# First norm in two VectorE operations and one of ScalarE a tile; last norm's sums gathered in PSUM

## The chip, the core and the metric

The kernel runs on one core of a Trainium2 chip. The metric is the device time of one execution in microseconds (us); of the kernel before three runs are shown. The core's engines run side by side, each through its own queue in program order: TensorE (PE; its weight loads are PEld), VectorE (DVE), ScalarE (ACT), GpSimd (POOL), and SyncE (SP), which here only issues DMAs. Matmul results land in PSUM, eight banks of 128 x 512 floats; everything else lies in SBUF.

## The reference

A decoder trunk of two layers over x (1024 tokens by 1024 channels, batch 1), conditioned by a vector c:

```python
c_act = jax.nn.silu(c)
for l in range(DEPTH):                                  # DEPTH = 2
    shift, scale, gate = jnp.split(c_act @ ada_w[l] + ada_b[l], 3, axis=-1)
    if l == 0:
        h = modulate(rmsnorm(x, norm_g[l]), shift, scale)   # h * (1 + scale) + shift
        y = pool_mixer(h, a_w_in[0], a_w_group[0], a_scale[0], a_w_out[0])
    else:
        kb, vb = shared_kv_blocks(x, c_act, kv_norm_g, kv_ada_w, kv_ada_b, w_kv)
        h = modulate(rmsnorm(x, norm_g[l]), shift, scale)
        y = swa_sink_mixer(h, kb, vb, pos_bias, mask, b_w_in[0], b_sinks[0], b_w_out[0])
    x = x + gate[:, None, :] * y
return rmsnorm(x, final_g)
```

`pool_mixer` projects h to u and z, takes causal means of u over 2, 4, 8 or 16 tokens by channel group, mixes each group by a matrix, gates with silu(z) and projects back. `swa_sink_mixer` is windowed attention with sinks. All is float32.

## The kernel before

x is kept transposed: channels on the 128 partitions, in eight tiles k (`xk[k]`), tokens along the row, in two halves q of 512. A float32 factor is split into a high part, rounded to fp32r, and a low part, the remainder; a product is three fp32r matmuls (high times high, high weight times low activation and so on), accumulated in PSUM.

The stage that the change touches is the head, up to 88.6 us. It has these parts.

- Joined weights. For the first channel group the input projection and the group matrix are multiplied on the chip beforehand (`join_mm`, `split_wg`, `split_wu`, loads `fetch_c`, four pieces c0 to c3). The eight 128 x 512 results lie in PSUM banks `jb[0..7]`; `joined_h` (ScalarE) and `joined_l` (VectorE) write their high and low parts to SBUF. For m = 2, 3, 6 and 7 `joined_raw` (ScalarE) copies the bank to SBUF and `joined_sub` (GpSimd) subtracts from the copy.
- Statistics. `square2` (ScalarE) and `add2` (VectorE, for three tiles GpSimd) sum the squares of x over k for each q, `fold` closes the sum. `rstd_stats` sums over the partitions on TensorE into bank "o", VectorE writes `v` (L144), GpSimd raises it to the power of -0.5 (L149), and `rstd_spread` (L156) spreads the factors over the partitions into bank "tp"; ScalarE copies them to `rbs[q]`.
- adaLN. `dots` multiplies and sums two 128 x 1024 tiles of `ada_w` with silu(c), spread over the partitions in `cact` (L241 on VectorE), for shift and scale of one k, and `mod_scale` (L260) joins scale and norm_g to a column of `acol`. The spreading of c is a matmul of a row of ones with c, split in two fp32r parts (`onesr`, `crow`, L453).
- Modulation and first matmuls. `first_xn` multiplies x by the norm factor (L179), `first_h` writes the high part of h on ScalarE (L161), h itself over x (L372) and the low part on GpSimd (L373); for k = 0 `soon_h` and `soon_l` do the last two on VectorE (L378, L383). `first_mm` (L396) is a block of twelve matmuls for one k and q: four with the high parts, four with the low weight, four with the low activation. There are sixteen blocks, in the order k = 0, 4, 1, 5, 2, 6, 3, 7. The banks of q = 0 are those of `jb[0..3]`, the others "tp", "o" and those of `jb[6..7]`.

In this stage the order of every engine's queue is that of the source (`manual_schedule` over all engines). The loads of SP are in the same order; a load into a tile in use waits, with all loads behind it.

After the head, `block_sums` (L612, L613, L615) forms sums and differences of the h tiles that the later products need, four a j, while TensorE runs the first gates (L216). Later stages touch none of the changed code but the last: there the output projection's last half is done in two quarters of 256 tokens, each followed by `stats_quarter`, which sums two partial squares (`sq` and `more`) with `rstd_stats`: two matmuls for `sq` (L140, each recorded as two passes), `v` (L144), two for `more`, an addition (L147), the power (L149). A tile `fill` of `CONST_FILL` columns lies behind the constants in SBUF.

## Time and profile before

| | us |
|---|---|
| median of 3 runs | 996.78 (995.62 to 997.03) |
| profiled execution | 997.35 |
| its span | 995.6 |
| TensorE busy in the span | 971.3 (98%) |
| VectorE busy | 784.8 (79%) |
| ScalarE busy | 468.2 (47%) |
| GpSimd busy | 178.9 (18%) |

The span runs from the first to the last instruction that the profile shows; the execution's time is a little longer. Busy shares are means over the whole span, and matmuls overlap, so a busy TensorE need not be at its peak. The granted clock of TensorE is 1.00 at 2.4 GHz and 0.50 at 1.2 GHz. In a row of the timeline the first number is the start, the second the duration; what stands in brackets is the idle time before it and what ended it. "PE ps_d" is a matmul into a bank of tag d.

### The profile page before, as it was taken

The page shows a single profiled execution, that of the slowest core. Times are in us where ns is not written, and L with a number is a line of the kernel's source. Part 1 is how long each engine was busy: PE and PEld are TensorE (multiplying, and loading weights), DVE is VectorE, ACT ScalarE, POOL GpSimd, SP SyncE. Part 2 cuts the span into 40 slices and gives each one's busy share as a digit, 9 for nine tenths or more (in the row PEclk, how much of TensorE's full clock was granted, in tenths as well). Part 3 has the DMA queues.
Part 4 walks back from the last instruction along what each step waited for, and adds up shares of the span by engine and source line. Part 5 has one row for each costly group of instructions (what it writes and reads, how often), then busy time and mean ns, then how long its engine had stood idle before and what let it go on. Part 6 is the DMA issues. An engine that isn't in the chain of part 4 may idle for free.

```text
span 995.6 us, 12704 instructions
## 1 busy us (share of the span) xinstructions
PE 971.3 (98%) x4530; PEld 801.7 (81%) x4530; DVE 784.8 (79%) x1405; ACT 468.2 (47%) x912; POOL 178.9 (18%) x194
## 2 busy tenths in 40 slices
PE   8899999999999999999999999999999999999996
PEld 6677888888888887888888886877788888887786
DVE  6998977767997699676782358699899878889995
ACT  6545534423343344551121134486767555666534
POOL 3652000000000000000000000043334212336723
PEclk9899999999999999999999999999999999999999
DMA  8462532164116410779871212412212221223222
GB/s 313 155 212 106 170 106 71 56 233 148 58 49 233 147 54 32 257 270 339 294 234 64 86 43 85 138 53 85 65 64 85 85 77 61 76 78 113 85 86 85
DMA packets 40625, 125.67 MB, mean 126 GB/s; under 512 B 4465, under 2 KB 6641, under 8 KB 40434
## 3 DMA queue, kind: packets, MB, share of 16 engines
q1 hardware_dynamic: 40416, 123.82, 36.8%
q10 hardware_dynamic: 146, 1.05, 0.3%
q8 instruction: 35, 0.57, 0.2%
q14 instruction: 28, 0.23, 0.1%
HBM read 111.22 MB, written 13.63 MB: 125 GB/s over the span
## 4 chain that ended last, share of the span: by engine, by line
PE 72%; DVE 20%; ACT 3%; issue 2%; POOL 1%; DMA 0%; POOLq 0%; DVEq 0%; SPq 0%; ACTq 0%
PE ps_d L216 13%; PE ps_d L657 10%; PE ps_S L216 8%; PE ps_d L207 5%; PE ps_d L205 5%; PE ps_d L206 5%; PE ps_S L657 4%; PE ps_o L216 4%; PE ps_tp L216 3%; DVE wl L121 3%; PE ps_o L657 2%; PE ps_tp L657 2%; PE ps_d L396 2%; DVE tmp L572 1%; DVE ad L241 1%
## 5 line engine op out<-in xcount | busy, mean ns | idle before, releaser
L119 ACT CAST wh<-raw 128x1024 fp32r<-128x1024 f32 x80 | 83.7, 1046 | 109.1 <-PE ps_d L216 66.6
L121 DVE TENSOR_TENSOR wl<-raw,wh 128x1024 fp32r<-128x1024 f32 x80 | 103.0, 1288 | 39.5 <-ACT wh L119 35.5
L205 PE MATMUL ps_d<-hm,wh 128*128 128x512 f32 x288 | 113.9, 396 | 1.1 <-ACT wh L119 1.1
L207 PE MATMUL ps_d<-hm,wl 128*128 128x512 f32 x288 | 112.7, 391 | 1.4 <-DVE wl L121 1.4
L206 PE MATMUL ps_d<-hm,wh 128*128 128x512 f32 x288 | 112.4, 390 | 0.0
L216 PE MATMUL ps_d<-gh,wh 128*128 128x512 f32 x224 | 82.1, 390 | 0.0
L241 DVE CUSTOM_DVE_ANT_0 tmp<-tmp,cact,pk 128x1024 f32<-128x1024 f32 x48 | 60.8, 1283 | 26.7 <-DMA tmp<-ada_rest 26.5
L207 PEld LDWEIGHTS ps_d<-hm,wl 128*128 128x128 f32 x288 | 54.1, 188 | 14.4 <-DVE wl L121 3.0
L216 PE MATMUL ps_S<-gh,wh 128*128 128x512 f32 x192 | 64.6, 390 | 0.0
L657 PE MATMUL ps_d<-hs,ws 128*128 128x512 f32 x264 | 64.0, 391 | 0.0
L205 PEld LDWEIGHTS ps_d<-hm,wh 128*128 128x128 f32 x288 | 54.1, 188 | 11.7 <-ACT wh L119 1.7
L1129 ACT ACTIVATE pt<-pt,nm 128x129 f32<-128x129 f32 x128 | 50.2, 395 | 26.5 <-DVE nm L1125 24.3
L206 PEld LDWEIGHTS ps_d<-hm,wh 128*128 128x128 f32 x288 | 54.2, 188 | 9.9
L657 PEld LDWEIGHTS ps_d<-hs,ws 128*128 128x128 f32 x264 | 49.6, 188 | 10.8
L564 POOL MEMSET tmp<- 128x16 f32 x16 | 1.7, 112 | 291.3 <-DVE tmp L572 129.7
L657 PE MATMUL ps_d<-ha,ws 128*128 128x512 f32 x216 | 52.9, 393 | 0.0
L633 ACT CAST ws<-tw 128x512 fp32r<-128x512 f32 x44 | 26.7, 621 | 54.7 <-PE ps_tp L216 15.2
L572 DVE TENSOR_TENSOR tmp<-tmp 128x1039 f32<-128x1039 f32 (+3 forms) x40 | 49.4, 1235 | 2.0 <-ACT tmp L693 0.9
L149 POOL TENSOR_TENSOR rs<-v,mhalf 128x4 f32<-128x4 f32 (+1 forms) x7 | 7.0, 996 | 237.3 <-DVE v L144 218.2
L216 PEld LDWEIGHTS ps_d<-gh,wh 128*128 128x128 f32 x224 | 42.0, 188 | 8.9
L657 PEld LDWEIGHTS ps_d<-ha,ws 128*128 128x128 f32 x216 | 40.7, 188 | 9.2
L216 PE MATMUL ps_d<-gh,wl 128*128 128x512 f32 x112 | 43.6, 390 | 0.0
(301 smaller groups left out, 2537.2 us busy)
## 6 DMA issues: line engine op xcount, KB each, us to landing
tmp<-ada_rest SPq DMA_DIRECT2D x48, 512.0 KB, 4.6
raw<-wb SPq DMA_DIRECT2D x32, 512.0 KB, 3.3
raw<-wa SPq DMA_DIRECT2D x28, 512.0 KB, 3.5
raw<-wao SPq DMA_DIRECT2D x20, 512.0 KB, 4.2
x<-xT SPq DMA_DIRECT2D x32, 256.0 KB, 6.0
ad<-ada_first SPq DMA_DIRECT2D x16, 512.0 KB, 4.4
raw<-wbo SPq DMA_DIRECT2D x16, 512.0 KB, 3.3
kept_g<-tmp SPq DMA_DIRECT2D x14, 512.0 KB, 2.8
```

What stands on the lines that cost most here:

```text
L119: nc.scalar.copy(out=wh, in_=raw)
L121: nc.vector.tensor_sub(out=wl, in0=raw, in1=wh.bitcast(F32))
L205: mm(ps, lh, acts(k, 0), start=k == 0, stop=False)
L206: mm(ps, lh, acts(k, 1), start=False, stop=False)
L207: mm(ps, ll, acts(k, 0), start=False, stop=k == n - 1)
L216: mm(p, lhs, acts(k, hl, q), start=start and k == 0 and s == 0, stop=stop and k == n - 1 and s == 2)
L241: nc.vector.tensor_tensor_reduce(out=raw, in0=raw, in1=ca, scale=0.5, scalar=pk[:, bcol:bcol + 1], op0=ALU.mult, op1=ALU.add, accum_out=ad ...
L396: mm(psu[i, q], w0[k // 2][:, k % 2, w, i * P:(i + 1) * P], block(k, q)[hl], start=k == 0 and s == 0, stop=k == KT - 1 and s == 2)
L572: nc.vector.tensor_add(out=nx[:, 2 * s - 1:], in0=cur[:, 2 * s - 1:], in1=cur[:, s - 1:PAD + T - s])
L633: nc.scalar.copy(out=ws[i][:, 0, :], in_=src)
L657: mm(ps, lhs, acts(k, hl), start=start and k == 0 and s == 0, stop=k == 3 and s == 2, skip_group_check=True)
L1129: nc.scalar.activation(pt[:, i, :P + 1], pt[:, i, :P + 1], AF.Exp, bias=nm[:, i:i + 1], scale=-1.0, accum_out=den[:, i:i + 1])
```

## The change

- `rstd_stats` with a second tile accumulates both groups of sums in the same PSUM columns; the addition of the second (L147) is gone.
- c is spread by one float32 matmul a half, from `ones` and `cact`; `crow` and `onesr` are gone.
- `joined_raw` and `joined_sub` are gone: all eight low parts of the joined weights are `joined_l` on VectorE. All additions of squares are on VectorE.
- The tile `xn` is gone. `first_h` multiplies x by the column of `acol` and by the norm factor in one VectorE operation, in place, and ScalarE adds the shift while rounding the high part. `first_l` adds the shift and subtracts the high part in one VectorE operation. What stays in x is h without its shift, so `block_sums` adds the shifts (columns of `adac`, and their sums in `acol[:, 24:28]`).
- The column of `acol` is made by ScalarE (Identity with scale and bias) instead of L260.
- Order: the loads of x tiles 4 to 7 of q = 0 come before those of c3, and `fetch_ada(0)` before the last four x tiles. The low parts and matmuls of a k stand one k later in the loop. `dots(4)` stand behind the second norm factor, and its spreading behind `first_mm(0, 0)`.
- `acol` has 28 columns and `CONST_FILL` is 44.

```diff
-CONST_FILL = 56
+CONST_FILL = 44
...
-    acol = cp.tile([P, 24], F32, name="acol")
+    acol = cp.tile([P, 28], F32, name="acol")
...
-        def sums(t, c0):
+        for i, t in enumerate((sq,) if more is None else (sq, more)):
             for j in range(n):
-                mm(st[:, c0 + j:c0 + j + 1], t[:, j * P:(j + 1) * P], invd, start=True, stop=True)
-
+                mm(st[:, j:j + 1], t[:, j * P:(j + 1) * P], invd, start=i == 0 and j == 0,
+                   stop=j == n - 1 and (i == 1 or more is None))
         v = sp.tile([P, 8], F32, tag="v", name="v")
-        sums(sq, 0)
         nc.vector.tensor_scalar_add(out=v[:, :n], in0=st[:, :n], scalar1=EPS)
-        if more is not None:
-            sums(more, n)
-            nc.vector.tensor_add(out=v[:, :n], in0=st[:, n:2 * n], in1=v[:, :n])
         rs = sp.tile([P, 8], F32, tag="rs", name="rs")
         nc.gpsimd.tensor_tensor(out=rs[:, :n], in0=v[:, :n], in1=mhalf[:, :n], op=ALU.pow)
...
-        crow = hp.tile([P, 2, T], F32R, tag="h", name="crow")
-        onesr = sp.tile([P, H], F32R, tag="xn", name="onesr", bufs=5)[:, :P]
-        nc.vector.tensor_copy(out=onesr[0:1, :], in_=ones[0:1, :].broadcast_to([1, P]))
...
-        def joined_raw(*ms):
...
-            for m in ms:
-                if m % 2 == 0:
-                    copies[m // 2] = tmp()
-                nc.scalar.copy(out=copies[m // 2][:, half(m % 2)], in_=jb[m])
...
-        def joined_sub(*ms):
-            for m in ms:
-                w = w0[m // 2][:, m % 2]
-                nc.gpsimd.tensor_sub(out=w[:, 1, :], in0=copies[m // 2][:, half(m % 2)],
-                                     in1=w[:, 0, :].bitcast(F32))
...
         def dots(k, i):
             ada_dot(ads[k][i], cact, 8 * i + k, C_ADAB + 8 * i + k)
             if i:
-                mod_scale(k, 8 + k, C_NG + k, 1)
-
-        xns = {}
-
-        def first_xn(k, q):
-            xns[k, q] = xn_tile(k, q, rbs[q])
+                g = pk[:, C_NG + k:C_NG + k + 1]
+                nc.scalar.activation(acol[:, k:k + 1], adac[:, 8 + k:9 + k], AF.Identity,
+                                     bias=g, scale=g)
...
         def first_h(k, q):
-            a, b, h, l = first_parts(k, q)
-            mod_h(xns[k, q], a, b, h)
-            nc.scalar.activation(first_f(k, q), xns[k, q], AF.Identity, bias=b, scale=a)
-            nc.gpsimd.tensor_sub(out=l, in0=first_f(k, q), in1=h.bitcast(F32))
-
-        def soon_h(k, q):
+
             a, b, h, _ = first_parts(k, q)
-            mod_h(xns[k, q], a, b, h)
-            nc.vector.tensor_scalar(out=first_f(k, q), in0=xns[k, q], scalar1=a, scalar2=b,
-                                    op0=ALU.mult, op1=ALU.add)
-
-        def soon_l(k, q):
-            _, _, h, l = first_parts(k, q)
-            nc.vector.tensor_sub(out=l, in0=first_f(k, q), in1=h.bitcast(F32))
+            nc.vector.scalar_tensor_tensor(out=first_f(k, q), in0=first_f(k, q), scalar=a,
+                                           in1=rbs[q], op0=ALU.mult, op1=ALU.mult)
+            nc.scalar.activation(h, first_f(k, q), AF.Identity, bias=b, scale=1.0)
+
+        def first_l(k, q):
+            _, b, h, l = first_parts(k, q)
+            nc.vector.scalar_tensor_tensor(out=l, in0=first_f(k, q), scalar=b,
+                                           in1=h.bitcast(F32), op0=ALU.add, op1=ALU.subtract)
...
-        def square2(n, q):
...
-        def add2(n, q, eng=None):
-            s = sq2[q][n % 2]
-            (eng or nc.vector).tensor_add(out=s, in0=s, in1=sqs[n, q])
+        def squares(q, *ks):
+
+            for n in ks:
...
+                nc.scalar.activation(sqs[n, q], xk[n][:, half(q)], AF.Square)
...
+        def adds(q, *ks):
+            for n in ks:
+                s = sq2[q][n % 2]
+                nc.vector.tensor_add(out=s, in0=s, in1=sqs[n, q])
...
             fetch_x(0, range(4))
             fetch_c(2)
+            fetch_x(0, range(4, 8))
             fetch_c(3)
-            fetch_x(0, range(4, 8))
-            fetch_x(1, range(8))
+            fetch_x(1, range(4))
             fetch_ada(0)
+            fetch_x(1, range(4, 8))
             fetch_ada(4)
...
-            nc.vector.tensor_copy(out=crow[0:1, 0, :], in_=cact[0:1, :])
-            nc.vector.tensor_sub(out=crow[0:1, 1, :], in0=cact[0:1, :],
-                                 in1=crow[0:1, 0, :].bitcast(F32))
             for i in range(3):
                 join_all(0, s=(i,))
             for q in range(2):
-                for i in range(2):
-                    mm(cbs[q], onesr[0:1, :], crow[0:1, i, half(q)], start=i == 0, stop=i == 1)
+                mm(cbs[q], ones[0:1, :].broadcast_to([1, P]), cact[0:1, half(q)],
+                   start=True, stop=True)
             split_wg(1)
             split_wu(1)
-            for k in range(4):
-                square2(k, 0)
-            for k in range(2, 4):
-                add2(k, 0)
+            squares(0, 0, 1, 2, 3)
+            adds(0, 2, 3)
...
+            squares(0, 4, 5, 6, 7)
+            adds(0, 4, 5, 6, 7)
+            squares(1, 0, 1, 2)
             join_all(3, (4, 5))
-            rs = rstd_stats(sq2[0][0], 4)
+            rs = rstd_stats(fold(0), 4)
             joined_h(4, 5)
             joined_l(4, 5)
-            square2(3, 1)
+            squares(1, 3)
             join_all(3, (0,))
-            add2(2, 1)
-            add2(3, 1, nc.gpsimd)
-            square2(4, 1)
+            adds(1, 2, 3)
             joined_h(0)
             join_all(3, (1,))
+            dots(0, 0)
+            joined_l(0)
             bc = rstd_spread(rs, 4)
-            square2(5, 1)
-            joined_l(0)
+            nc.scalar.copy(out=rbs[0], in_=bc)
             joined_h(1)
-            add2(4, 1)
-            add2(5, 1, nc.gpsimd)
-            nc.scalar.copy(out=rbs[0], in_=bc)
+            squares(1, 4, 5)
+            dots(0, 1)
             join_all(3, (2, 3))
-            square2(6, 1)
+            adds(1, 4, 5)
             joined_l(1)
-            square2(7, 1)
-            dots(0, 0)
-            add2(6, 1, nc.gpsimd)
+            squares(1, 6, 7)
+            adds(1, 6, 7)
+            sq = fold(1)
+            first_h(0, 0)
             joined_h(2, 3)
-            joined_raw(2, 3)
-            dots(0, 1)
-            add2(7, 1)
-            fold(1)
-            joined_sub(2)
+            joined_l(2, 3)
+            first_l(0, 0)
             jb += [bank("S") for _ in range(2)]
             for ci in range(4):
                 join_mm(6, jb[6], ci)
             for ci in range(3):
                 join_mm(7, jb[7], ci)
-            first_xn(0, 0)
-            soon_h(0, 0)
-            rs = rstd_stats(sq2[1][0], 4)
-            soon_l(0, 0)
+            rs = rstd_stats(sq, 4)
             joined_h(6)
-            joined_raw(6)
-            joined_sub(3)
-            dots(4, 0)
-            dots(4, 1)
             join_mm(7, jb[7], 3)
+            first_mm(0, 0)
             bc = rstd_spread(rs, 4)
-            first_mm(0, 0)
             nc.scalar.copy(out=rbs[1], in_=bc)
-            first_xn(0, 1)
-            soon_h(0, 1)
+            joined_l(6)
             joined_h(7)
-            joined_raw(7)
-            soon_l(0, 1)
-            joined_sub(6, 7)
+            joined_l(7)
+            first_h(0, 1)
+            first_l(0, 1)
             first_mm(0, 1)
+            late = [0]
             for k in (4, 1, 5, 2, 6, 3, 7):
                 if k == 3:
                     first_raw = fetch(wa[16])
                 if k != 4:
                     last_load = fetch_ada(k)
-                    dots(k, 0)
-                    dots(k, 1)
+                dots(k, 0)
+                dots(k, 1)
                 for q in range(2):
-                    first_xn(k, q)
+                    if k != 4:
+                        first_l(late[0], q)
+                        first_mm(late[0], q)
                     first_h(k, q)
-                    first_mm(k, q)
+                late[0] = k
+            for q in range(2):
+                first_l(7, q)
+                first_mm(7, q)
...
             f11, f21, f12, f22 = [first_f(4 * c + j, q) for c in range(2) for q in range(2)]
-            add, sub = nc.vector.tensor_add, nc.vector.tensor_sub
-            sums = ((0, add, f22, f21, f22), (2, sub, f21, f11, f21),
-                    (1, sub, f11, f22, f11), (3, sub, f12, f12, f11))
-            for i, op, s, a, b in sums:
-                op(out=s, in0=a, in1=b)
+            b1, b2, bs = adac[:, j:j + 1], adac[:, 4 + j:5 + j], acol[:, 24 + j:25 + j]
+            if j == 0:
+                nc.vector.tensor_add(out=acol[:, 24:28], in0=adac[:, 0:4], in1=adac[:, 4:8])
+
+            add, sub = ALU.add, ALU.subtract
+            parts = ((0, f22, f21, bs, f22, add, add), (2, f21, f11, None, f21, None, sub),
+                     (1, f11, f22, b1, f11, sub, sub), (3, f12, f12, b2, f11, add, sub))
+            for i, s, a, shift, b, op0, op1 in parts:
+                if shift is None:
+                    nc.vector.tensor_tensor(out=s, in0=a, in1=b, op=op1)
+                else:
+                    nc.vector.scalar_tensor_tensor(out=s, in0=a, scalar=shift, in1=b, op0=op0,
+                                                   op1=op1)
                 nc.scalar.copy(out=sum_part(i, j, 0), in_=s)
-            for i, _, s, _, _ in sums:
-                sub(out=sum_part(i, j, 1), in0=s, in1=sum_part(i, j, 0).bitcast(F32))
+            for i, s, *_ in parts:
+                nc.vector.tensor_sub(out=sum_part(i, j, 1), in0=s,
+                                     in1=sum_part(i, j, 0).bitcast(F32))
```

TensorE's queue around the first block of first_mm. `ps_o<-invd,second` are the sums of the second half's squares, `ps_tp<-ident,rs` is rstd_spread, `ps_d<-ha` is first_mm(0, 0), and the rows after it first_mm(0, 1). Before:

```order
L140 MATMUL ps_o<-invd,second 128x1 x4
L309 MATMUL ps_S<-wgs,wu 128x512 x3
L156 MATMUL ps_tp<-ident,rs 128x128 x4
L396 MATMUL ps_d<-ha,w_127 128x512 x12
L396 MATMUL ps_tp<-a_432,w_127 128x512
L396 MATMUL ps_o<-a_432,w_127 128x512
```

And now:

```order
L140 MATMUL ps_o<-invd,second 128x1 x4
L301 MATMUL ps_S<-wgs,wu 128x512 x3
L365 MATMUL ps_d<-ha,w_124 128x512 x12
L152 MATMUL ps_tp<-ident,rs 128x128 x4
L365 MATMUL ps_tp<-a_416,w_124 128x512
L365 MATMUL ps_o<-a_416,w_124 128x512
```

The spreading of the second half's factors moved from ahead of the first block to behind it.

VectorE's queue from the fold of the second half's squares (`second<-second`) to the first products of the loop. `v` belongs to the second half's statistics, `ISA ad` is a dot of adaLN, `w_..<-ps` is joined_l. Before:

```order
L415 TENSOR_TENSOR second<-second 128x512
L179 TENSOR_TENSOR xn<-x,second 128x512
L378 TENSOR_SCALAR x<-xn,acol,adac 128x512
L144 TENSOR_SCALAR v<-ps_o 128x4
L383 TENSOR_TENSOR ha<-x,ha 128x512
L241 ISA ad,adac<-ad,cact,pk 128x1024
L241 ISA adac 128x1
L241 ISA ad,adac<-ad,cact,pk 128x1024
L241 ISA adac 128x1
L260 SCALAR_TENSOR_TENSOR acol<-adac,pk 128x1
L179 TENSOR_TENSOR xn<-x,second 128x512
```

And now:

```order
L387 TENSOR_TENSOR second<-second 128x512
L345 SCALAR_TENSOR_TENSOR x<-x,acol,second 128x512
L311 TENSOR_TENSOR w_125<-ps_d,w_125 128x512 x2
L351 SCALAR_TENSOR_TENSOR ha<-x,adac,ha 128x512
L143 TENSOR_SCALAR v<-ps_o 128x4
L311 TENSOR_TENSOR w_127<-ps_S,w_127 128x512 x2
L345 SCALAR_TENSOR_TENSOR x<-x,acol,second 128x512
L351 SCALAR_TENSOR_TENSOR a_416<-x,adac,a_416 128x512
L233 ISA ad,adac<-ad,cact,pk 128x1024
L233 ISA adac 128x1
L233 ISA ad,adac<-ad,cact,pk 128x1024
L233 ISA adac 128x1
```

Four joined_l stand between the fold and the second half's first product (L345), and the two dots of k = 4 moved from ahead of that product to behind it.

The loads that SP issues at the start, where `wgr` and `raw` are the pieces of the joined weights and `x` the tiles of x. Before:

```order
L285 DMA x<-xT 128x512 x4
L278 DMA wgr<-wg 128x512
L281 DMA raw<-wu 128x1024
L278 DMA wgr<-wg 128x512
L281 DMA raw<-wu 128x1024
L285 DMA x<-xT 128x512 x12
L290 DMA ad<-ada_first 128x1024 x12
```

And now:

```order
L277 DMA x<-xT 128x512 x4
L270 DMA wgr<-wg 128x512
L273 DMA raw<-wu 128x1024
L277 DMA x<-xT 128x512 x4
L270 DMA wgr<-wg 128x512
L273 DMA raw<-wu 128x1024
L277 DMA x<-xT 128x512 x4
L282 DMA ad<-ada_first 128x1024 x2
L277 DMA x<-xT 128x512 x4
```

Four loads of x moved ahead of the last piece, and two of `ada_first` ahead of the last four of x.

## Rows read from the trace of the kernel before

**Rows 1.** The page's first part: an engine, its busy time in us, the share of the span, and its instructions.

```profile
PE 971.3 (98%) x4530; PEld 801.7 (81%) x4530; DVE 784.8 (79%) x1405; ACT 468.2 (47%) x912; POOL 178.9 (18%) x194
```

**Rows 2.** TensorE's waits between 20 and 90 us: what waited, for what, us in total, times, the longest.

```profile
PE ps_o L140 <- DVE second L415: 2.7, 1, 2.7
```

**Rows 3.** Windows of 1 us: length, busy time and instructions of PE, PEld, DVE, ACT and POOL, then the granted clock (PEclk), the DMA share and GB/s.

```profile
32.00:33.00 1.00, 0.85 (x4) 0.38 (x2) 1.00 (x1) 0.00 (x0) 0.69 (x1) 1.00 0.51 106
...
35.00:36.00 1.00, 0.47 (x3) 0.51 (x3) 0.98 (x2) 0.00 (x0) 0.00 (x0) 0.50 0.78 291
...
41.00:42.00 1.00, 1.00 (x4) 0.81 (x4) 0.97 (x3) 0.59 (x1) 1.00 (x1) 0.59 0.87 340
```

**Rows 4.** The timeline of all engines in the head: start us, duration us, engine, line, operation.

```profile
12.44 0.73 PE L453 MATMUL ps_tp<-crow,onesr 1*128 1x512 f32 x2
...
13.57 3.04 PE L309 MATMUL ps_d<-wgs,wu 128*128 128x512 f32 x12
...
17.39 1.06 ACT L302 CAST wu<-raw 128x1024 fp32r<-128x1024 f32 x1 [1.12 <-DMA raw<-wu]
...
23.25 0.95 PE L140 MATMUL ps_o<-invd,first 128*128 128x1 f32 x8
...
24.24 0.17 DVE L144 TENSOR_SCALAR v<-ps_o 128x4 f32<-128x4 f32 x1 [1.24 <-PE ps_o L140]
...
25.56 1.16 PE L156 MATMUL ps_tp<-ident,rs 128*128 128x128 f32 x8
...
28.29 1.07 ACT L314 CAST w<-ps_d 128x512 fp32r<-128x512 f32 x2
...
34.69 0.69 DVE L415 TENSOR_TENSOR second<-second 128x512 f32<-128x512 f32 x1
...
37.64 1.41 POOL L149 TENSOR_TENSOR rs<-v,mhalf 128x4 f32<-128x4 f32 x1 [4.96 <-DVE v L144]
...
39.11 2.07 PE L156 MATMUL ps_tp<-ident,rs 128*128 128x128 f32 x8 [0.25 <-POOL rs L149]
```

**Rows 5.** VectorE's timeline over one turn of the loop, in the same columns.

```profile
51.89 1.29 DVE L179 TENSOR_TENSOR xn<-x,second 128x512 f32<-128x512 f32 x2
53.10 1.28 DVE L241 CUSTOM_DVE_ANT_0 ad<-ad,cact,pk 128x1024 f32<-128x1024 f32 x1
...
54.30 2.32 DVE L241 CUSTOM_DVE_ANT_0 ad<-ad,cact,pk 128x1024 f32<-128x1024 f32 x1
...
56.66 1.12 DVE L260 SCALAR_TENSOR_TENSOR acol<-adac,pk 128x1 f32<-128x1 f32 x1
57.71 1.28 DVE L179 TENSOR_TENSOR xn<-x,second 128x512 f32<-128x512 f32 x2
```

**Rows 6.** Pieces of the chain that ended last: start us, us, what (the last line is of the tail).

```profile
29.01 0.60 DVE w L319
...
53.48 3.32 PE ps_d L396 x12
...
88.59 0.23 PE ps_d L216
...
99.55 0.23 PE ps_d L216
...
962.21 0.66 DVE x L1260
```

**Rows 7.** Groups of instructions by line and form, the first two over the whole span, the last from 52 to 125 us: busy us, mean ns of one, then idle time before them.

```profile
L913 DVE SCALAR_TENSOR_TENSOR tmp<-x,acol,rb 128x512 f32<-128x512 f32 x16 | 11.8, 746 | 0.0
...
L915 ACT ACTIVATE hm<-tmp,adac 128x512 fp32r<-128x512 f32 x16 | 11.6, 726 | 13.0 <-DVE tmp L913 12.9
...
L612 DVE TENSOR_TENSOR x<-x 128x512 f32<-128x512 f32 x12 | 8.3, 691 | 0.3
```

**Rows 8.** Windows of other stretches, with the columns of rows 3.

```profile
0.00:12.00 12.00, 9.30 (x27) 7.16 (x28) 6.39 (x9) 6.21 (x10) 3.99 (x24) 1.00 0.75 256
12.00:18.00 6.00, 6.00 (x26) 4.42 (x25) 4.11 (x6) 4.64 (x8) 2.95 (x2) 1.00 0.97 325
...
24.00:29.00 5.00, 5.00 (x27) 4.13 (x28) 4.76 (x7) 4.88 (x11) 3.90 (x3) 1.00 1.01 404
...
88.00:100.00 12.00, 12.00 (x54) 9.88 (x53) 11.06 (x18) 4.20 (x8) 0.11 (x1) 1.00 0.61 220
100.00:130.00 30.00, 30.00 (x133) 24.61 (x132) 29.48 (x44) 14.28 (x24) 0.22 (x2) 1.00 0.58 193
```

**Rows 9.** The timeline of TensorE, VectorE and ScalarE around the two last statistics, in the columns of rows 4.

```profile
975.28 0.50 PE L140 MATMUL ps_o<-invd,sqq 128*128 128x1 f32 x4
976.18 0.58 PE L140 MATMUL ps_o<-invd,sqq 128*128 128x1 f32 x4 [0.39 <-ACT x L1226]
...
988.17 0.16 DVE L147 TENSOR_TENSOR v<-ps_o,v 128x2 f32<-128x2 f32 x1 [0.76 <-PE ps_o L140]
...
987.56 0.58 PE L140 MATMUL ps_o<-invd,sqq 128*128 128x1 f32 x4 [0.41 <-DVE v L144]
...
986.85 0.42 ACT L1222 ACTIVATE sqq<-x 128x256 f32<-128x256 f32 x1 [0.62 <-DVE x L1212]
```

**Rows 10.** The load of x tiles issued by SP from 16 to 20 us (duration of the issue in ns, first and last start), and of those from 18.5 to 20.5 us the count, size and median us from issue to landing.

```profile
L285 SPq DMA_DIRECT2D x<-xT x6: 328/328/593, 15.6 to 20.0; - x6
...
x<-xT SPq DMA_DIRECT2D x3, 256.0 KB, 5.1
```

More of the change, by code (lines that the diff above doesn't have):

```diff
@@ L397, in first_mm @@
                    start=k == 0 and s == 0, stop=k == KT - 1 and s == 2)
+        sq2 = [[t[:, 1, half(i)] for i in range(2)] for t in (first_t, second_t)]
         sqs = {}
-        def square2(n, q):
-            if n < 2:
-                sqs[n, q] = sq2[q][n]
-            elif n % 2 == 0:
-                t = tmp()
-                sqs[n, q], sqs[n + 1, q] = t[:, half(0)], t[:, half(1)]
-            nc.scalar.activation(sqs[n, q], xk[n][:, half(q)], AF.Square)
-        def add2(n, q, eng=None):
-            s = sq2[q][n % 2]
-            (eng or nc.vector).tensor_add(out=s, in0=s, in1=sqs[n, q])
+        def squares(q, *ks):
+            for n in ks:
+                if n < 2:
+                    sqs[n, q] = sq2[q][n]
+                elif n % 2 == 0:
+                    t = tmp()
+                    sqs[n, q], sqs[n + 1, q] = t[:, half(0)], t[:, half(1)]
+                nc.scalar.activation(sqs[n, q], xk[n][:, half(q)], AF.Square)
[3 more added lines that the diff above has]
+                nc.vector.tensor_add(out=s, in0=s, in1=sqs[n, q])
         def fold(q):
             nc.vector.tensor_add(out=sq2[q][0], in0=sq2[q][0], in1=sq2[q][1])
+            return sq2[q][0]
         ET = mybir.EngineType
```

7 lines of the change are left out of this document (removed).

## The prediction

> **What bounds the kernel now.** I read the page first: TensorE is busy 98% of the span [rows 1], so the end moves only where TensorE waits or runs slowly. The waits of TensorE between 20 and 90 us [rows 2] name the place: 2.7 us for a sum of squares (L415), in the first norm, and little else. But the clock is part of it: TensorE idles from 32.85 us on, its granted clock is halved (1.2 GHz) by 35 us, and 2.4 GHz come back between 41 and 42 us [rows 3]. The timeline then shows why that sum is late [rows 4]: from 24.24 us VectorE works without a gap down to 35.38 us. GpSimd is part of the reason: a dot product (L241) takes 1.28 us by itself and 2.3 us beside a GpSimd subtraction, and the L260 on a single column takes 1.12 us [rows 5]. In the loop over the other seven k tiles VectorE repeats every 5.80 us (51.89, 57.71) [rows 5], while TensorE needs 24 matmuls. Their unhindered pitch is read one stage later in the chain of waits: 48 from 88.59 to 99.55 us, 0.2283 us each [rows 6], so 5.48 us a k. VectorE bounds the loop by a little. Behind 88.6 us TensorE is full [rows 8] and a shift of the head passes on. In the tail the end is a chain of small waits between VectorE, TensorE and GpSimd [rows 9].
>
> **The change, part by part.** The sum is made in the span of the profiled execution, 995.6 us; that execution took 997.35 us, 1.75 more than its span and 0.57 more than the median, 996.78.
>
> *A, up to the first statistics.* The removed copies of c (onesr, crow) are VectorE work beside a busy TensorE: nothing. Their four fp32r matmuls took from 12.44 to 13.57 us, 1.1 us [rows 4]; now there are two in float32. No 512-column float32 matmul stands in the trace. Below: the same four passes at the pitch of 0.23 us, 0.9. Above: the 128-column ones (L156, two passes each, eight passes in 1.16 us, so 0.145 a pass [rows 4]) grown with their columns, four passes of 4 x 0.145, 2.3 us. I take 1.9, nearer the row of the same type, so +0.8 us on TensorE's queue. The larger effect is the order of loads. The last piece of the joined weights (wg3, wu3) now stands behind four more tiles of x. Up to its last byte the queue then holds 5.31 MB (5184 KiB), where 4.26 MB stood before. By 12 us 12 x 256 = 3.07 MB have come [rows 8]; the full rate is 404 GB/s [rows 8], so the last byte comes at 12 + 2.24/0.404 = 17.5 us. A landing is 1.1 us later than such a count: the last x tile (7.41 MB) is counted at 24.0 and landed at 20.0 + 5.1 = 25.1 us [rows 10]. So wu3 lands at 18.6 us, where its cast began at 17.39 [rows 4]. Bounds: 17.4, and 20.0 at the 325 GB/s of 12 to 18 us. Behind the cast the same queues follow (cast, four squares, four adds, fold), 5.86 us to the statistics matmuls at 23.25, which now start at 24.5 and end at 25.4, not 24.2: **+1.2**. The +0.8 on TensorE hides beneath this (23.41 + 0.8 = 24.2); without that cover it would count.
>
> *B, to the second sum of squares.* VectorE now does, in the order shown: eleven 128x512 operations at a pitch of 0.605 us (0.60 for L319 in the chain [rows 6], a little more with the hand-off) and two dots at 1.20 with 0.1 for the accumulator, 6.66 + 2.5 = 9.2, and v 0.1. GpSimd has only its power left. 25.4 + 9.3 = 34.7 us, against 35.38: the stretch shrinks from 11.1 to 9.3 although three adds come over from GpSimd.
>
> *C, to the steady loop.* Here the new order costs. Modulation goes from the sum through first_h (VectorE 0.7 us; scalar_tensor_tensor has a pitch of 0.66 [rows 6]), ScalarE (0.73, as L915 [rows 7]) and, queued behind it on ScalarE, two casts of PSUM (1.07 for two [rows 4]): 37.2 us. The second joined_l 0.7: 37.9; before, ScalarE copies freed these PSUM banks earlier. first_l 0.65, then v: 38.7. GpSimd's power, 1.0 to 1.4 [rows 4]: 39.8. Meanwhile TensorE had the last bank at 37.95 and needs nine more matmuls: 40.0. The spreading matmuls (L156 before) now stand behind this first block; 1.16: 41.2. Copy 0.59, cast of bank 7 0.6, its joined_l 0.7, first_h 0.7, ScalarE 0.73: 44.6 with the hand-offs, where the second block starts. Then VectorE: first_l 0.7, two dots 2.5, ScalarE's 128x1 0.25, first_h 0.7, ScalarE 0.73: 49.6 us for the third block, later than before because the dots of k = 4 were done before the second norm factor and now come behind it. Its last four matmuls want first_l(4,0), behind the dots of k = 1: 48.8 + 0.7 + 2.5 + 0.7 = 52.7, plus 0.9, plus a block of 2.74: the fifth block starts at 56.4, against 53.48 [rows 6]: **+2.9** where it was -0.7.
>
> *D, the loop.* Per k VectorE now has two dots, 2.5, and four scalar_tensor_tensor at 0.66: 5.14 us, below the 5.48 of TensorE, which becomes the bound. Twelve blocks of twelve matmuls at 0.2283: 32.9 us, against 35.1 (53.48 to 88.59 [rows 6]): **-2.2**. The low parts are computed one k behind, 0.6 us and more ahead of their use. The stage ends at 89.3 us, **+0.7 us** for A to D.
>
> *E, block sums.* Twelve of sixteen additions become scalar_tensor_tensor, 0.747 for 0.691 us (L913 and L612 [rows 7]): 0.7 us on VectorE beneath a TensorE that is full from 88 to 130 us [rows 8]: 0, and +0.7 without that cover. The 128x4 add is 0.16 at most.
>
> *F, last norm.* The second group of sums no longer waits for v. First quarter: TensorE starts it at 976.18 and could at 975.28 + 0.50 = 975.78 [rows 9]: -0.4, passed on since L1212 waits for TensorE. Last quarter: 987.56 becomes 987.3 when the square ends (986.85 + 0.42): -0.25. The removed 128x2 add costs nothing, as the remaining one takes its place in the chain [rows 9]. **-0.65**; from 0 (another wait steps in) to -1.
>
> Sum: +0.7 - 0.65 = +0.05: a span of 995.65, as an execution 997.4, as a median **996.8 us**: no change.
>
> **Rivals.** *The loop's gain alone (faster).* If the long wait of C overlaps more than I think, so that the loop starts no later than before, -2.2 - 0.65 remain: 993.9. For it: VectorE idles for 5.6 us in C by my own sum (1.4 for the casts, 3.1 for the spreading, 0.8 and 0.3 for ScalarE), and a few queue positions less would give them back. Against: queues are in order, and the spread stands behind twelve matmuls in the program. Chance 0.18.
>
> *The clock falls early (slower).* TensorE is thinly used from 34 to 38 us (statistics, three join matmuls, three of the first block), waiting for joined_l; before, 2.7 us of idling brought half clock for over 6 us [rows 3]. At half clock the nine matmuls take 2.05 us more, the spread 0.9 more (2.07 against 1.16 [rows 4]), all in the chain of C: +3.0, 999.8 us. It decides if the granted clock is at half before 38 us. Against: in these 4 us TensorE is busy more than half the time. A later fall, in the idling from 41.3 to 44.6, costs nothing: the second block would run at half clock to 50.1, the third waits for first_l until 52.7 anyway; only a clock that is still low at 54 us costs about 1. Chance 0.15. The Trainium skill (TensorE: Matmul & The Clock Gate, Part 1: The HAM clock gate) holds that half rate is the default and only activity releases it, and that the place where it flips moves from run to run; the rows agree on the two levels, and by that rule the later fall is to be expected and the early one possible.
>
> *The weights land late (slower).* wu3 at 20.0 or later moves the whole head by 1.4 us and more: 998.2 to 999.4. For: the same load landed 2 us behind its byte count before (4.26 MB is counted at 12 + 1.19/0.325 = 15.7, the cast began at 17.39). Against: ScalarE and TensorE have other work until 17. Chance 0.17.
>
> **How the numbers follow.** The forecast has 0.5, with its own range of 996.0 to 998.9 (landing between 17.4, where the +0.8 of TensorE steps in and leaves -0.4, and 20.0; tail between 0 and -1). A measurement of this kernel tells 0.2%, 2 us, from no change. Faster by more: most of the first rival and a little of the forecast, 0.2. Slower by more: the clock, half of the late landing and a little of the forecast, 0.28. Same: 0.52. The range of 994.0 to 1000.2 reaches to the first and second rival.
>
> **What would show it.** Right: the first statistics end near 25.4 us, the second fold near 34.7, the second block starts near 44.6 and the fifth near 56.4, TensorE runs the loop at 5.5 us a k with no waits for first_l, and the stage ends near 89.3; no dot takes over 1.3 us. In the tail the second group of sums follows the first at once. Wrong: a fold before 33 us, a loop that starts before 54 us, a granted clock at half before 38 us, a loop period above 5.6 us, or a wait behind 90 us that was not there.

## The result, and the profile after

The changed kernel takes 998.45 us in the median of 22 runs (996.47 to 1000.63), the kernel before 996.76 us on the same chip (22 runs, 994.98 to 998.12). The ratio is 1.0019 with an interval of 1.0013 to 1.0026: slower by 1.9 us (1.3 to 2.6), clear of the noise but just below the 0.2%, 2 us, that the forecast had set as the bound of no change. It said 996.8 us.

The profiled execution is the longest of the 22: 1000.63 us, a span of 998.9 us, 2.2 us above the median. Part of what it shows is therefore its own, and the experiments have to say how much. The page's first part, busy time by engine:

```profile
PE 971.9 (97%) x4530; PEld 804.0 (80%) x4530; DVE 775.5 (78%) x1412; ACT 458.3 (46%) x902; POOL 143.2 (14%) x173
```

Against [rows 1], VectorE lost 9.3 us of work, ScalarE 9.9 and GpSimd 35.7, and yet the span grew by 3.3 us. TensorE, the bound, has the same 4530 matmuls. TensorE's waits from 20 to 92 us (what waited, for what, total, times, longest):

```profile
PE ps_tp L365 <- ACT a L347: 3.3, 1, 3.3
PE ps_d L365 <- ACT ha L347: 2.1, 1, 2.1
PE ps_o L140 <- DVE second L387: 0.8, 1, 0.8
PE ps_d L365 <- DVE w L311: 0.2, 1, 0.2
```

The wait for the sum of squares that [rows 2] had at 2.7 us is down to 0.8 (L387), and two new ones stand ahead of the second block (3.3) and the third (2.1). The chain of waits from 14 to 100 us shows what lay between (start, us, what):

```profile
14.32 4.54 PE ps_d L301 x12
18.86 1.37 PE ps_S L301 x6
20.23 2.72 PE ps_d L301 x12
22.95 2.72 PE ps_S L301 x12
25.67 0.80 PE ps_o L140 x8
...
35.10 0.69 DVE second L387
...
38.46 4.33 PE ps_d L365 x10
42.79 0.91 PE ps_tp L152 x8
...
44.83 0.69 DVE w L311
45.52 0.67 DVE x L345
...
46.21 0.73 ACT a L347
...
52.14 4.59 PE ps_d L365 x12
...
59.45 2.72 PE ps_d L365 x12
...
92.35 0.23 PE ps_d L212
```

Twelve matmuls take 2.72 us at 20.23 and 4.54 at 14.32; ten of the first block (38.46) take 4.33, twelve of the third (52.14) 4.59. The windows of 1 us say why; the columns are those of [rows 3], and the granted clock is the third number from the end:

```profile
14.00:15.00 1.00, 1.00 (x4) 0.65 (x4) 0.70 (x2) 0.74 (x3) 0.00 (x0) 0.89 1.05 406
15.00:16.00 1.00, 1.00 (x4) 0.81 (x3) 0.67 (x1) 1.00 (x2) 0.47 (x1) 0.50 1.07 412
...
38.00:39.00 1.00, 0.77 (x2) 0.19 (x1) 1.00 (x3) 0.66 (x2) 0.00 (x0) 0.84 0.00 0
39.00:40.00 1.00, 1.00 (x3) 0.83 (x3) 1.00 (x4) 0.00 (x0) 0.19 (x1) 0.50 0.00 0
...
52.00:53.00 1.00, 0.86 (x2) 0.69 (x3) 1.00 (x1) 0.75 (x2) 0.00 (x0) 0.67 0.95 332
53.00:54.00 1.00, 1.00 (x4) 0.78 (x3) 1.00 (x3) 0.00 (x0) 0.00 (x0) 0.50 0.19 78
```

TensorE is at 1.2 GHz three times: behind the two float32 spreading matmuls of c (12.34 to 14.3), in the first block, and in the third. Before there was one such stretch, 35 to 41 us [rows 3]. The groups of the loop (32 to 92 us; busy us, mean ns, then idle time before them):

```profile
L233 DVE CUSTOM_DVE_ANT_0 ad<-ad,cact,pk 128x1024 f32<-128x1024 f32 x15 | 18.7, 1277 | 0.0
L345 DVE SCALAR_TENSOR_TENSOR x<-x,acol,second 128x512 f32<-128x512 f32 x16 | 11.8, 743 | 0.5 <-ACT acol L317 0.5
...
L317 ACT ACTIVATE acol<-adac,pk 128x1 f32<-128x1 f32 x8 | 3.1, 387 | 13.9 <-DVE adac L233 13.9
```

All fifteen dots take 1.28 us; in [rows 5] one took 2.32 beside GpSimd. From the fifth block to the stage's end the chain needs 92.35 - 59.45 = 32.9 us, 5.48 a k, and the list above has no wait of TensorE in that stretch: TensorE bounds the loop. In the tail the last two groups of sums and v (timeline, columns of [rows 4]):

```profile
989.99 0.58 PE L140 MATMUL ps_o<-invd,sqq 128*128 128x1 f32 x4 [0.63 <-DVE sqq L1193]
...
990.74 0.61 PE L140 MATMUL ps_o<-invd,sqq 128*128 128x1 f32 x4 [0.17 <-ACT sqq L1191]
...
991.46 0.16 DVE L143 TENSOR_SCALAR v<-ps_o 128x2 f32<-128x2 f32 x1 [1.22 <-PE ps_o L140]
```

The second group now waits for its square, no longer for v as in [rows 9]. The stage end is 3.76 us later than before and the span 3.3 longer, so the tail gave back some 0.46 (the spans are rounded to 0.1).

### The profile page after: what moved, and what is told of

Read it like the earlier page. It is cut to its first block, busy times and chain, and to the rows that moved or that the text cites. A ratio compares the mean times of both kernels' runs of the same rounds, so it can differ in the third digit from the quotient of the medians.

```text
span 998.9 us, 12673 instructions
## 1 busy us (share of the span) xinstructions
PE 971.9 (97%) x4530; PEld 804.0 (80%) x4530; DVE 775.5 (78%) x1412; ACT 458.3 (46%) x902; POOL 143.2 (14%) x173
## 3 DMA queue, kind: packets, MB, share of 16 engines
q10 hardware_dynamic: 146, 1.05, 0.3%
## 4 chain that ended last, share of the span: by engine, by line
PE 75%; DVE 17%; ACT 3%; issue 2%; POOL 1%; DMA 1%; POOLq 0%; DVEq 0%; SPq 0%; ACTq 0%
PE ps_d L212 13%; PE ps_d L626 9%; PE ps_S L212 8%; PE ps_d L203 6%; PE ps_d L201 6%; PE ps_d L202 6%; PE ps_S L626 4%; PE ps_o L212 4%; PE ps_tp L212 3%; DVE wl L121 3%; PE ps_d L365 3%; PE ps_tp L626 2%; PE ps_o L626 2%; DVE tmp L532 1%; PE ps_d L301 1%
## 5 line engine op out<-in xcount | busy, mean ns | idle before, releaser
L212 PEld LDWEIGHTS ps_S<-gh,wh 128*128 128x128 f32 x192 | 35.9, 188 | 7.4
```

Of the source, the lines that this page charges most:

```text
L212: mm(p, lhs, acts(k, hl, q), start=start and k == 0 and s == 0, stop=stop and k == n - 1 and s == 2)
```

## The experiments

The theory at this point: the structure forecast is right (weights 1.2 us later, a slow start of the loop, a faster loop, a shorter tail), and the excess is half clock, in the front and in two blocks. The rivals: the order of loads costs more than forecast; the new order of the modulation costs more than forecast without any clock; the matmuls of c in float32 are the loss by themselves. Each ratio is against the kernel before, and 0.001 is 1.0 us.

**e2_loads: the changed kernel, with the loads in the order of before.**

```diff
             fetch_c(2)
-            fetch_x(0, range(4, 8))
             fetch_c(3)
-            fetch_x(1, range(4))
+            fetch_x(0, range(4, 8))
+            fetch_x(1, range(8))
             fetch_ada(0)
-            fetch_x(1, range(4, 8))
```

> The changed kernel with the loads in the order of the kernel before (the last piece of the joined weights ahead of x tiles 4 to 7). Theory of the prediction (late weights set the first statistics): they end 1 us earlier and the ratio falls to 1.001. Theory A (TensorE's own queue sets them, through the single-partition float32 matmuls and the clock behind them): the cast of the last weights begins near 17.4 us, not 18.5, but the statistics still end near 26 us and the ratio stays at 1.002.

Measured 996.82 us (11 runs, 995.99 to 1001.07), ratio 1.0007 (0.9997 to 1.0018): 1.2 us of the 1.9 are gone, as much as the prediction had counted for the loads, though the intervals overlap. The cast of wu3 began at 17.32 us and the first statistics at 23.23, so theory A's late statistics did not come in this execution. Windows of its trace:

```profile
12.00:18.00 6.00, 6.00 (x23) 4.04 (x22) 3.67 (x5) 3.94 (x7) 2.98 (x2) 1.00 0.95 313
...
44.00:45.00 1.00, 1.00 (x4) 0.77 (x4) 1.00 (x2) 0.00 (x0) 0.00 (x0) 0.58 0.00 0
45.00:46.00 1.00, 1.00 (x4) 0.81 (x3) 1.00 (x3) 0.00 (x0) 0.00 (x0) 0.50 0.00 0
```

Here the clock held behind the matmuls of c, and fell only behind the second block's 3.3 us wait. The third block ran at full rate and waited 0.83 us for first_l. From the second fold's end (33.95) to the fifth block (55.83) there are 21.9 us, where the changed kernel's profile had 23.7 and the forecast 21.7. One execution thus shows step C without the clock's part. (The fold's end is the end of the L387 row of `second`, the fifth block's start that of the chain, here and below.)

**e1_crow: the changed kernel, with c again spread in two fp32r parts.** **e9_before_f32: the kernel before, with the float32 spreading alone**, the same edit the other way round.

```diff
+            nc.vector.tensor_copy(out=crow[0:1, 0, :], in_=cact[0:1, :])
+            nc.vector.tensor_sub(out=crow[0:1, 1, :], in0=cact[0:1, :],
+                                 in1=crow[0:1, 0, :].bitcast(F32))
...
-                mm(cbs[q], ones[0:1, :].broadcast_to([1, P]), cact[0:1, half(q)],
-                   start=True, stop=True)
+                for i in range(2):
+                    mm(cbs[q], onesr[0:1, :], crow[0:1, i, half(q)], start=i == 0, stop=i == 1)
```

> The changed kernel with c spread again by four fp32r matmuls from a split row (crow, onesr). Theory A: the two float32 matmuls on a single partition cost TensorE 0.8 us themselves and bring its clock down to half from 14.9 to 18.1 us, which costs 1.7 us more; so here the granted clock stays at 1.00 between 12 and 20 us, the first statistics end near 25.1 us (where the late weights set them) and not 26.5, and the ratio to the kernel before is 1.0005 or so, not 1.0019. Rival: the clock falls there from the phase of the run alone or the loads set the time; then the statistics still end after 26 us and the ratio stays at 1.002.

> The kernel before with one edit of the change: c spread by two float32 matmuls on one partition. Theory A: TensorE's queue sets the first statistics there, so they are 0.8 us later, and in some executions the clock falls behind them and costs 1.7 us more; ratio 1.0008 to 1.002. Rival: the edit is hidden and the ratio is 1.0000.

e1_crow measured 997.5 us (11 runs, 997.18 to 999.26), ratio 1.0011 (1.0002 to 1.0020); e9_before_f32 997.65 us (11 runs, 995.69 to 999.69), ratio 1.0008 (0.9999 to 1.0018). Both put the float32 spreading at 0.8 us, each with an interval of about 1 us to either side, so the size is poorly known: the interval of e9 still takes in its rival's 1.0000, and that of e1 reaches the changed kernel's 1.0019. In the trace of e1_crow the clock held in the front and the first statistics start at 23.49 us. The trace of e9_before_f32, the timeline first:

```profile
12.08 1.12 PE L445 MATMUL ps_tp<-cact,ones 1*128 1x512 f32 x2
...
13.04 1.02 PE L445 MATMUL ps_o<-cact,ones 1*128 1x512 f32 x2
...
25.26 0.95 PE L140 MATMUL ps_o<-invd,first 128*128 128x1 f32 x8
```

and its windows of 1 us:

```profile
13.00:14.00 1.00, 1.00 (x4) 0.20 (x2) 0.27 (x2) 0.60 (x1) 0.00 (x0) 1.00 1.04 418
14.00:15.00 1.00, 1.00 (x4) 0.82 (x4) 0.83 (x2) 0.90 (x2) 0.00 (x0) 0.63 1.01 391
15.00:16.00 1.00, 1.00 (x3) 0.79 (x3) 0.42 (x1) 1.00 (x2) 0.72 (x1) 0.50 1.03 387
```

The fall from the changed kernel's front appears in the kernel before with these two matmuls alone, and its first statistics start at 25.26 us, not 23.25 [rows 4], though wu3 had landed early (cast at 16.57) and the sum of squares was complete at 23.17. Over all profiles, the clock fell there in three of the seven kernels that spread c in float32 (the changed one, e9_before_f32, e10_fill_all) and in none of the six that don't (before, e1, e5, e6, e7, e11). With one profile a kernel that points to these matmuls; it does not prove that only they bring the fall.

**e3_spread and e4_spread_dots: the changed kernel, with VectorE's v ahead of the joined low parts and the spreading matmuls ahead of the first block**; e4 also puts the two dots of k = 4 ahead of the second half's first product, where they were before.

```diff
             first_h(0, 0)
-            joined_h(2, 3)
-            joined_l(2, 3)
-            first_l(0, 0)
...
             rs = rstd_stats(sq, 4)
+            joined_h(2, 3)
+            joined_l(2, 3)
+            first_l(0, 0)
...
-            first_mm(0, 0)
             bc = rstd_spread(rs, 4)
+            first_mm(0, 0)
...
             joined_h(7)
+            dots(4, 0)
+            dots(4, 1)
```

The last two added lines, with the dots in the loop then left out for k = 4, are in e4_spread_dots alone.

> As e4, but with the dots of k = 4 left where the change has them, behind the second half's product: only v and the spreading are moved forward. Theory B: of the 4.6 us that e4 gained against the changed kernel most comes from the spreading; by the sum of the prediction the second block starts 3.1 us after the changed kernel's place less, some 6.8 us behind the second fold, and the third block then waits for the dots; ratio 0.998 to 0.999. Rival: the two moves count alike, as the third block's wait stays; ratio 1.000.

> The changed kernel with three places of its order undone: v of the second statistics right behind first_h(0, 0), the spreading of the factors ahead of first_mm(0, 0), and the dots of k = 4 ahead of the second half's product. Theory B (the new order from the second fold to the third block costs 2.9 us): the distance from the second fold to the fifth block falls from 22.0 to some 18.3 us, the stage ends 3 to 4 us earlier, ratio 0.998 to 0.999. Rival: the lost time is the clock's; then the waits move, the clock is at half as long as before in this stretch, and the ratio stays above 1.0005.

e3_spread measured 996.24 us (11 runs, 994.25 to 997.37), ratio 0.9989 (0.9980 to 0.9998); e4_spread_dots 993.85 us (8 runs, 993.04 to 995.02), ratio 0.9973 (0.9963 to 0.9983). So 3.0 us come back with v and the spread, whose parts were not tried apart, and 1.6 more with the dots, 4.6 of a kernel that had lost 1.9. The timeline of TensorE in e4_spread_dots:

```profile
36.89 1.68 PE L152 MATMUL ps_tp<-ident,rs 128*128 128x128 f32 x8 [0.54 <-POOL tmp L526]
38.22 4.20 PE L365 MATMUL ps_d<-ha,w 128*128 128x512 f32 x12
43.33 0.50 PE L365 MATMUL ps_tp<-a,w 128*128 128x512 f32 x1 [0.91 <-ACT a L347]
```

The first block is at half clock here too (4.20 us), but nothing waits behind it: the spread had gone ahead, so copy, joined_l and first_h of the second half ran beside it, and the second block waits 0.9 us, not 3.3. The trace of e6_all (below), with the same order here, shows the first block at full rate:

```profile
38.97 3.00 PE L369 MATMUL ps_d<-ha,w 128*128 128x512 f32 x12
...
44.06 0.50 PE L369 MATMUL ps_tp<-a,w 128*128 128x512 f32 x1 [2.10 <-ACT a L351]
```

There the second block starts 8.95 us behind the second fold's end (35.11), in e4_spread_dots too (43.33 less 34.38): with this order the half clock of the first block cost nothing. From the second fold's end to the fifth block there are 18.1 us (34.38 to 52.45), as in the kernel before (35.38 to 53.48).

**e11_before_late_spread: the kernel before, with the spreading matmuls behind the first block**, nothing else.

```diff
-            bc = rstd_spread(rs, 4)
             first_mm(0, 0)
+            bc = rstd_spread(rs, 4)
```

> The kernel before with one edit: the spreading of the second half's factors behind first_mm(0, 0), as in the change. Theory B: the second block and with it VectorE's loop start some 3 us later (a block at half clock, 4 to 5 us, less the 0.8 us that VectorE's dots had covered): ratio 1.002 to 1.004. Rival: VectorE bounds the loop anyway and has work meanwhile; ratio 1.000.

Measured 998.2 us (11 runs, 996.29 to 1000.21), ratio 1.0015 (1.0006 to 1.0024): slower, though by less than was expected. Fold to fifth block takes 20.0 us (34.78 to 54.76), 1.9 more than before. TensorE in its timeline:

```profile
38.05 4.34 PE L396 MATMUL ps_d<-ha,w 128*128 128x512 f32 x12
42.22 1.05 PE L156 MATMUL ps_tp<-ident,rs 128*128 128x128 f32 x8
45.52 0.51 PE L396 MATMUL ps_tp<-a,w 128*128 128x512 f32 x1 [2.25 <-ACT a L161]
```

The order of two lines makes a half-clock block part of the path, in a kernel that has none of the change's other edits. It costs less than e3_spread gave (1.5 for 3.0 us). The traces suggest why: the kernel before had a late spread to begin with, 3.7 us behind the fold's end (39.11 [rows 4] less 35.38), where e3_spread has 2.5 (37.08 less 34.56). Of these 1.2 us the second statistics at half clock are 0.8 (1.84 us for 1.02) and GpSimd's power 0.4 (1.41 [rows 4] for 1.01).

**e8_fill and e10_fill_all: the changed kernel, with matmuls that do no work put into TensorE's gaps**: e8 ahead of the second statistics, of the first block and of the second block (their results land in banks that the blocks then overwrite); e10 also ahead of the third block, where they add zeros.

```diff
+            new_psu(0)
+            fill(psu[0, 0], 3)
             rs = rstd_stats(sq, 4)
...
+            fill(psu[0, 0], 3)
             first_mm(0, 0)
...
+            fill(psu[1, 1], 11)
             first_mm(0, 1)
...
+                    if (k, q) == (1, 0):
+                        for _ in range(7):
+                            mm(psu[0, 0][:, :P], zero[:, :1].broadcast_to([P, P]), ident,
+                               start=False, stop=False)
```

> The changed kernel with filler matmuls (128 x 128 float32, into banks that are free) on TensorE: three ahead of the second statistics, three ahead of the first block, eleven ahead of the second block, so that TensorE idles less from 34 to 47 us; nothing else is moved. Theory C (what the forecast missed is the clock, which falls inside the first block in some executions): the granted clock stays at 1.00 from 34 to 47 us in the profile, the first block takes 2.8 us and not 4.3, the median falls by 1 to 2 us, ratio 1.000 to 1.001, and the times spread less. Rival: the fillers stand in the way or the clock was not what cost; ratio 1.002 or above.

> As e8, and seven more fillers (a column of zeros spread over 128, added to a bank in use, so nothing changes in it) ahead of the third block, where TensorE still idled for 2.1 us in e8. Theory C (the clock in the first blocks is what the sum of the prediction missed in its part C): the granted clock stays at 1.00 from 33 to 57 us, the third block takes 2.8 us and not 4.8, the ratio falls to 1.0005 to 1.001. Rival: the waits set the third and fourth block whatever the clock; the ratio stays at 1.0016.

e8_fill measured 998.55 us (11 runs, 996.29 to 1000.44), ratio 1.0016 (1.0005 to 1.0028): nothing gained that can be told, and the times did not spread less, as had been expected. e10_fill_all measured 997.6 us (11 runs, 996.35 to 998.35), ratio 1.0009 (1.0000 to 1.0018): 1.0 us gained, with intervals that overlap a little. In the trace of e8_fill the first block was at full rate (twelve matmuls in 3.22 us, where ten took 4.33 in the changed kernel), but the third was not; its windows:

```profile
50.00:51.00 1.00, 1.00 (x5) 0.79 (x6) 1.00 (x3) 0.54 (x1) 0.00 (x0) 0.94 0.70 250
51.00:52.00 1.00, 1.00 (x4) 0.81 (x3) 1.00 (x1) 0.00 (x0) 0.00 (x0) 0.50 0.53 164
```

With that gap filled too, the clock held from 18 to 57 us. The end of the second fold and the third block in the timeline of e10_fill_all:

```profile
34.57 0.69 DVE L396 TENSOR_TENSOR second<-second 128x512 f32<-128x512 f32 x1
...
50.23 2.09 PE L374 MATMUL ps_d<-ha,w 128*128 128x512 f32 x8 [0.54 <-ACT ha L348]
53.22 1.20 PE L374 MATMUL ps_d<-ha,w 128*128 128x512 f32 x4 [0.89 <-DVE ha L352]
```

and the fifth block in its chain:

```profile
57.14 2.72 PE ps_d L374 x12
```

Its last four matmuls wait for first_l (L352), the wait that step C had named, and fold to fifth block takes 21.9 us (35.26 to 57.14). So in these traces the clock is the difference between 23.7 and 21.9 us, and the order of the queues the other 3.8 down to 18.1; with half clock in the third block alone (e8_fill) it is 22.5. The rival of an order that costs more by itself falls: with the clock held, step C's sum stands.

**e5_tail: the kernel before, with the last norm's sums gathered in PSUM alone.**

```diff
+                mm(st[:, j:j + 1], t[:, j * P:(j + 1) * P], invd, start=i == 0 and j == 0,
+                   stop=j == n - 1 and (i == 1 or more is None))
...
-            sums(more, n)
-            nc.vector.tensor_add(out=v[:, :n], in0=st[:, n:2 * n], in1=v[:, :n])
```

> The kernel before with the change to the last norm alone (both groups of sums in the same PSUM columns). By the prediction's step F the last 22 us of the span shrink by 0.65 us: 0.4 in the first quarter's statistics, 0.25 in the last; ratio 0.9993. Rival: another wait steps in and nothing is gained, ratio 1.0000.

Measured 995.81 us (11 runs, 994.57 to 997.14), ratio 0.9991 (0.9982 to 0.9999): 0.9 us faster. Its tail shows the same three rows as the changed kernel's, the second group 0.18 us behind its square.

**e6_all and e7_all_loads: the repairs together.** e6 is the changed kernel with the edits of e1 and e4; e7 has the load order of e2 as well.

```diff
-            fetch_x(1, range(4))
+            fetch_x(0, range(4, 8))
+            fetch_x(1, range(8))
...
+                    mm(cbs[q], onesr[0:1, :], crow[0:1, i, half(q)], start=i == 0, stop=i == 1)
...
             bc = rstd_spread(rs, 4)
+            first_mm(0, 0)
...
+            dots(4, 0)
+            dots(4, 1)
```

The first three lines are in e7_all_loads alone.

> As e7, but with the loads in the order of the change. Theory A with the late weights: the last weights land near 18.5 us instead of 17.4 and set the first statistics, so 0.5 to 1 us are lost against e7: ratio 0.9962 to 0.9968. Rival: the load order is hidden and the ratio is e7's 0.9957.

> The changed kernel with everything undone that was found to cost: c spread by fp32r matmuls, the loads in the order of before, v and the spreading moved forward, the dots of k = 4 ahead. What stays is the modulation in two VectorE operations, the work off GpSimd and the gathered sums. If the gains add up (e4 0.9973, e1 0.0008, e2 some 0.0008): 0.9957 to 0.9965, and the first statistics end near 24.2 us. Rival: the first statistics and the second fold are not on the path any more; then 0.9973 as e4.

e6_all measured 994.18 us (9 runs, 992.78 to 995.35), ratio 0.9974 (0.9964 to 0.9984), short of what was expected and no better than e4_spread_dots: here the fp32r spreading gained nothing that can be told, where it had gained 0.8 in e1_crow with the same late weights. The two intervals allow both; why they differ was not tried. e7_all_loads measured 992.63 us (5 runs, 991.44 to 993.31), ratio 0.9957 (0.9944 to 0.9969): 4.3 us faster than the kernel before and, by the ratios, 6.2 faster than the changed one. The load order alone is 1.7 us between the two, where e2_loads gave 1.2. The head of e7_all_loads in the timeline:

```profile
16.98 1.05 ACT L298 CAST wu<-raw 128x1024 fp32r<-128x1024 f32 x1 [0.21 <-DMA raw<-wu]
...
23.32 1.05 PE L140 MATMUL ps_o<-invd,first 128*128 128x1 f32 x8 [0.22 <-DVE first L391]
```

and two pieces of its chain:

```profile
52.07 2.72 PE ps_d L369 x12
...
84.97 0.23 PE ps_d L212
```

The stage ends at 84.97 us, 3.6 us ahead of the kernel before [rows 6], with the loop's 32.9 us and a start that costs no more than before.

## Why the prediction was right, and where it was not

The forecast of no change came within 1.7 us of the median, inside its range; the interval of the ratio says that the change does cost something. The range held in part by luck: its upper end, 998.9, was room for weights that land later than forecast and a tail that gives nothing, and neither happened; the clock, which did fall, had been left to a rival. Step by step:

**A, the front: right in its main term, wrong in its cover.** wu3 was to be cast at 18.6 us and was at 18.55. The way from there to the statistics was taken as 5.86 us; where the clock held (e1, e3, e4, e6, e8) it was 5.64 to 5.66. In the kernel before it was not the weights that came last but TensorE's own queue, which has no wait ahead of its statistics in [rows 4]; so it was in e5 and e11, where the cast began at 15.91 and 16.24 us and the statistics at 22.60 and 22.66. The statistics of the five kernels with the late weights start at 23.5 to 24.7 us, in the mean 1.2 later than the 22.6 to 23.3 of the five undisturbed fronts with the old order of loads (before, e2, e5, e7, e11). What failed is "The +0.8 on TensorE hides beneath this". The matmuls cost what was estimated (12.34 to 14.3 us, 1.9), and where the clock held they did hide: in e3_spread TensorE still waited 0.61 us for the sum of squares.

```profile
24.17 1.05 PE L140 MATMUL ps_o<-invd,first 128*128 128x1 f32 x8 [0.61 <-DVE first L387]
```

But in some executions the clock falls behind them, and TensorE is then the late one: in the profile of the changed kernel the next twelve take 4.54 us, the chain is TensorE alone from 14.32 to 26.47 us, and the statistics start at 25.51. That is 1.0 later in this execution than the 24.5 of the forecast; in the medians the edit is worth about 0.8 (e1, e9).

**B: right.** From v (26.49) to the second fold's end (35.79) it took 9.3 us, as forecast, and no dot took over 1.28 us.

**C: the mechanism right, the clock underrated.** 21.7 us were forecast from the fold to the fifth block (34.7 to 56.4); with no cost of the clock there are 21.9 (e10, e2), in the profiled execution 23.7. By places: the second block 11.2 us behind the fold (forecast 9.9, and 9.8 in e10 and e2), the third 5.2 behind that (5.0 and 5.2), the fifth 7.3 behind the third (6.8 and 6.9). The first and the last excess are the two blocks at half clock. From the forecast's 21.7 to the 18.1 of e4_spread_dots there are 3.6 us; the ratios give 4.6, which would be these 3.6 and about 1.0 for the half clock.

**D: right.** 32.9 us, TensorE without a wait in it; the -2.2 is real, and e7 keeps it.

**E: right.** TensorE was busy for all of 92 to 134 us, so the longer block sums cost nothing.

**F: right.** -0.46 in the profile and -0.9 (-0.1 to -1.8) in e5_tail's times, for -0.65.

**The rivals.** *The clock falls early* did not decide by its own condition (half before 38 us): 0.84 were granted in 38 to 39 us and 0.50 only from 39 on. But half of its working came true, one microsecond late: ten matmuls of the first block took 4.33 us, 2.1 more than at 0.2283 each, as priced, of which 1.4 reached the second block (11.2 against 9.8 us behind the fold), while the spread behind it ran at full rate (1.05 us). The sentence that a fall between 41.3 and 44.6 costs nothing held in the trace of e2_loads; the clause behind it, that a clock still low at 54 us costs about 1, is what the third block paid (0.4 us, from 6.9 to 7.3, and 0.6 in e8_fill). The rule cited from the Trainium skill there (TensorE: Matmul & The Clock Gate, Part 1: The HAM clock gate), that the place of the flip moves from run to run, goes with the traces: of the five kernels with the changed kernel's front (the changed one, e3, e4, e8, e10) the clock fell there in the profiles of two. *The weights land late* did not happen: the cast of wu3 began at 17.8 to 19.1 us in the seven profiles with the new order, below its 20.0. *The loop's gain alone* is not this kernel, but it is e4_spread_dots: the steps that it would have had to skip are queue positions, and moving them gave 993.85 us, where it had said 993.9. So close a match is partly luck: in e4's profile the fifth block starts at 52.45 us, 1.0 earlier than before, where the rival had it no later.

**What stays open.** The 1.9 us divide into the forecast's own near-zero sum, about 1.0 for half clock in the blocks (e10) and about 0.8 for the float32 spreading (e1, e9). The two add up, but each interval is about as wide as the term, e6_all shows nothing of the second, and one profile a kernel cannot say in how many executions the clock fell. The mean granted clock of every execution is on record as well. In e8_fill the times go with it (996.29 us at 0.998, 1000.44 at 0.991); in the 22 executions of the changed kernel they do not (998.04 us at 0.989, 1000.63 at 0.993), so what spreads those times is not shown. Nor was it tried whether the float32 matmuls with all 128 rows would keep the clock.

## What to carry to other kernels

A change that takes 55 us of work off three engines gained nothing in time because, in queues that are served in order, a short dependent chain (v, spread, copy, first product) was written behind twelve matmuls and two dots: look at what stands ahead of each link of such a chain before counting what is saved. Where TensorE is fed through such gaps, price the blocks behind a gap at both clocks, and put long blocks where nothing waits for their end. Compare terms over several executions: the start of the cast of wu3 varied by 1.5 us over the six profiles with the old order of loads (15.91 to 17.39).

## What the runs showed of the hardware

- The granted clock fell to half while TensorE was counted busy without a gap, behind two float32 matmuls whose operands lie on one partition (15 to 18 us in the changed kernel, 14 to 18 in e9_before_f32). The other falls, that of [rows 3] and those in the blocks, came behind waits or gaps of TensorE.
- Two 1x512 float32 matmuls of this kind take 1.9 us together; no row of the kernel before had a price for them, and the estimate from [rows 4] (1.9) held.
- ScalarE needs 0.39 us for an activation on a single column (L317), not the 0.25 taken in step C.
